# Softmax normalisation of the latent-attention heads: from the score tiles to the gate tile

## The chip, the cores and the metric

The kernel runs on one core of one Trainium2 chip. A time is the device time of one execution in microseconds (us); the number given for a kernel is the median over its runs. A profile comes from one execution whose instructions the hardware profiler recorded; its span runs from the first instruction to the end of the last, and that execution's own device time stands beside it. The engines are named as in the profile: PE is the matrix engine (PEld its weight loads), DVE the vector engine, ACT the scalar engine, POOL is GpSimd, and SP issues transfers. The letter q behind an engine's name marks its instruction queue.

## The reference, cut to what matters

The model is an encoder of two layers on 512 tokens of width 1024. The first layer is a neighbourhood attention. The second is a latent attention with 16 heads, in which every query attends to all 512 keys, and whose output is multiplied by a gate before the output projection:

```python
def block_attention(q, k, v):                 # q, k: (B, S, H, 96); v: (B, S, H, 64)
    ...
    s = jnp.einsum('bqhd,bkhd->bhqk', qblk, k).astype(jnp.float32) * scale
    pr = jax.nn.softmax(s, axis=-1).astype(v.dtype)
    return jnp.einsum('bhqk,bkhd->bqhd', pr, v)

def mixer_mla(xn, w_in, q_norm, w_qb, kv_norm, w_kvb, w_out):
    c_q, c_kv, k_rope, z = jnp.split(xn @ w_in, ...)
    ...
    o = block_attention(q, k, v)
    return (o.reshape(B, S, H * MLA_V) * jax.nn.silu(z)) @ w_out
```

The softmax divides each row of exponentials by its sum. That sum belongs to one query and one head, so dividing the scores, dividing the head's output, or dividing the gate of that head and query all give the same product.

## The kernel before, in words

Everything is 32-bit. A matrix product is made of three products of rounded operands: each operand is split into a high part (a copy rounded on ACT) and a remainder (a subtraction on DVE or POOL). `mms` (line 123) issues such matmuls, `split` (lines 110 and 112) makes the two parts of a tile that comes out of a matmul or a transpose, and `load_w` (lines 99 to 101) loads a weight tile with a transfer on SP, makes the high part on ACT and the remainder on POOL, or on DVE where the caller asks for it.

The second layer's attention is `mla_heads`. It first makes the eight gate tiles `zs[j]` of 128 x 512 (`z_phase`, silu on ACT at line 190). Tile j has the 128 output columns of the head pair j as partitions and the 512 tokens as columns: partitions 0 to 63 belong to the even head, 64 to 127 to the odd head. Then it walks through 70 steps. Step i below 64 is one score tile: head i // 4, query block i % 4, so that a head pair is eight steps. In a step come, in this order,

- `score(i)`: three matmuls into a PSUM tile (bank "S"), the negated row maximum on DVE (line 1052), the exponential on ACT with the row sums accumulated (line 1054), the reciprocal of the sums on DVE (line 1055) and the product of the 128 x 512 tile `ex` with that reciprocal on POOL (line 1056);
- pieces of preparation for later heads (`queries`, `keys`, `values`, `rope`, weight loads), and in the last pair a second product of the layer (`ple`, whose tiles are stored to DRAM at line 1138);
- `turn(i - 3)`: four transposes of an older `ex` (line 155) and their split into `pt_hi` and `pt_lo`;
- in two of four steps `output(h, s)`: the matmuls of the head's values with the turned scores (line 1071), a whole head being done in step 4h + 9. Then `half_of` (lines 220 and 221) puts the two halves of the PSUM tile together in the tile `u` of the pair, and after the odd head `gated` multiplies `u` by `zs[j]` on POOL (line 225), copies the high part on ACT (line 228) and makes the remainder on POOL (line 229). These are `o1h` and `o1l`.

The output projection (`out_proj`) is the next stage. It runs through the pairs in chunks of two, the last pair in the last chunk, and reads its weights (`mla_o`), the residual rows (line 1251) and the norm's gains (line 148) by transfers on SP.

A score tile `ex` has four buffers, `u` two, the raw weight tiles three, the split weight tiles three. The order of PE's work is written by hand: each piece of a step is issued behind the last matmul of the piece before it (`issue_after`). On the other engines and on SP the order is planned when the program is built, with a timeline that estimates when each operand is there; on the chip each engine's queue then runs strictly in that order.

Of the kernel before, what the change touches and what calls it, by code (L numbers as in the profile page):

```python
# [13 lines left out]
F32 = mybir.dt.float32  # L14
F32R = mybir.dt.float32r
AF = mybir.ActivationFunctionType
ALU = mybir.AluOpType
AX = mybir.AxisListType
PSUM = bass.MemoryType.PSUM
P = 128  # L20
S = 512
# [19 lines left out]
class InOrder:  # L41

    def __init__(self, tc, engine):
        self.tc, self.engine, self.last = tc, engine, None
# [12 lines left out]
class Trunk:  # L57
    def __init__(self, tc, ctx, a, dbg=None):
        self.tc, self.nc, self.a = tc, tc.nc, a
        self.dbg = dbg or {}  # L60
        nc = self.nc
        ec = ctx.enter_context
        self.act, self.dve = nc.scalar, nc.vector
        self.const = ec(tc.tile_pool(name="const", bufs=1))
        self.big = ec(tc.tile_pool(name="big", bufs=8))
        self.zp = ec(tc.tile_pool(name="zp", bufs=8))
        self.wp = ec(tc.tile_pool(name="wp", bufs=4))
        self.ps = ec(tc.tile_pool(name="ps", bufs=2, space=PSUM))
        self.half = self.const.tile([P, 1], F32, name="half")
        self.ident = self.const.tile([P, P], F32, name="ident")  # L70
        nc.vector.memset(self.half, -0.5)
        self.small = ec(tc.tile_pool(name="small", bufs=8))
        self.rows = [[self.const.tile([P, NT], F32, name=f"row{n}{l}") for n in "abcd"] for l in range(2)]
        self.wx, self.wxn = None, 0
        dram = ec(tc.tile_pool(name="dram", bufs=4, space=bass.MemoryType.DRAM))
        self.spill = [dram.tile([P, D], F32, name=f"spill{t}") for t in range(NT)]
        self.pe = [[dram.tile([P, D], F32, name=f"pe{l}{t}") for t in range(NT)] for l in range(2)]
        self.quarter = {}
        self.sums = [{p: dram.tile([2 * P, D], F32, name=f"sum{l}{p}") for p in (4, 5, 6, 7)} for l in range(2)]

    def bigtile(self, name):
# [860 lines left out]
    def mla_heads(self, pool, xT, cT, sets, oT):  # L942


        nc, a = self.nc, self.a
# [90 lines left out]
                self.split(dst[0][r], dst[1][r], psk[r])  # L1036
            A["k", j] = self.last_copy

        EX, ST, PT, U = {}, {}, {}, {}

        def score(i):
            h, qt = i // 4, i % 4
            st = sets[h // 2 % 2]
            q, k, kk = ((st["qe"], st["ke"], 96), (st["qo"], st["ko"], 128))[h % 2]
            if qt == 0:
                ST[h] = [self.small.tile([P, 4], F32, name=n, tag=n) for n in ("mx", "sm", "rc")]
            mx, sm, rc = (t[:, qt:qt + 1] for t in ST[h])
            sp = self.psum("S")
            Q = lambda s: q[s][0:kk, qt * P:(qt + 1) * P]
            K = lambda s: k[s][0:kk, :]  # L1050
            self.mms(sp, [(Q(0), K(0)), (Q(0), K(1)), (Q(1), K(0))])
            nc.vector.reduce_max(mx, sp, axis=AX.X, negate=True)  # L1052
            ex = EX[i] = pool.tile([P, S], F32, name="ex", tag="ex", bufs=4)
            nc.scalar.activation(ex, sp, AF.Exp, bias=mx, accum_out=sm)  # L1054
            nc.vector.reciprocal(rc, sm)  # L1055
            nc.gpsimd.tensor_tensor(out=ex, in0=ex, in1=rc.to_broadcast([P, S]), op=ALU.mult)  # L1056

        def turn(i):
            h, qt = i // 4, i % 4
# [80 lines left out]
        zs = self.z_phase(a["mla_z"], xT, range(NEARLY))  # L1140
# [11 lines left out]
        for i in range(70):  # L1152
            work = []
            if i < 64:
                work.append(lambda: score(i))
                work += pieces(i // 8)[i % 8]
            elif i < 68:
                work.append(ple)
            if 3 <= i < 67:
                work.append(lambda: turn(i - 3))  # L1160
            if i >= 8 and i % 4 < 2:
                work.append(lambda: output(i // 4 - 2, i % 4))
            for f in work:
                with self.tc.issue_after(self.last_mm.ins):
                    f()
            if i == 53:
                last = self.last_mm
# [307 lines left out]
```

## Time and profile before

| | us |
|---|---|
| median of 3 runs | 653.36 |
| lowest and highest run | 652.73, 653.73 |
| the profiled execution's own time | 653.56 |
| its span | 651.5 |

The mean granted clock of PE in the profiled execution was 0.995. The page of the profile gives the busy time of each engine, the span in 40 slices, the transfers, the chain of work that ended last, and the costliest groups of instructions: line, engine, operation, output and inputs, count, then busy time, mean duration of one, and the idle time of the engine just before them with what ended it. Other views answer for a stretch of the span: who waited for whom, an engine's instructions in order of time (start, duration, engine, line), or the busy time of each engine in several stretches.

### The profile page before, as it was taken

Reading aid. Unit: us, or ns where it says so; the run is one execution under the profiler, and the core shown is the slowest. Engines: PE = TensorE matmul, PEld = TensorE weight load, DVE = VectorE, ACT = ScalarE, POOL = GpSimd, SP = SyncE. Lnnn points to the kernel's source line nnn. Section 1 sums busy time; section 2 is a strip of 40 time slices with the busy share of each in tenths; the row PEclk is TensorE's granted clock in tenths of the full one; section 3 lists DMA queues with packets and bytes.
Section 4 is the critical chain, followed back from the end, with each engine's and each line's share of the span. In section 5 each row is a group of like instructions: output and inputs, shape, how many; then the busy total and the mean of one; then the engine's idle time right before and its main releaser. Section 6 shows DMA issues by size and latency. Waiting matters only on the chain.

```text
span 651.5 us, 9980 instructions
## 1 busy us (share of the span) xinstructions
PE 640.2 (98%) x3299; PEld 541.9 (83%) x3299; DVE 427.7 (66%) x886; ACT 453.4 (70%) x903; POOL 408.4 (63%) x371
## 2 busy tenths in 40 slices
PE   9999999999999999999999999999999999999994
PEld 6888878888888888888999887888888888888884
DVE  6197987565665616569715514898988885474665
ACT  7575766887886733788644535897989897547855
POOL 0471006877978853797655516786969887437974
PEclk9999999999999999999999999999999999999997
DMA  9939725778958989446643245120112223683524
GB/s 326 355 124 306 217 66 179 263 205 217 229 209 217 239 178 342 147 154 188 224 140 102 78 109 156 32 75 24 49 50 66 65 84 112 229 292 126 193 65 162
DMA packets 46131, 107.41 MB, mean 165 GB/s; under 512 B 4736, under 2 KB 17792, under 8 KB 46080
## 3 DMA queue, kind: packets, MB, share of 16 engines
q1 hardware_dynamic: 34608, 87.12, 39.3%
q0 software_dynamic: 11040, 18.88, 13.6%
q10 hardware_dynamic: 432, 0.79, 0.3%
q8 instruction: 26, 0.43, 0.3%
q14 instruction: 25, 0.20, 0.1%
HBM read 95.23 MB, written 25.17 MB: 185 GB/s over the span
## 4 chain that ended last, share of the span: by engine, by line
PE 83%; POOL 1%; ACT 1%; DVE 0%; DMA 0%; issue 0%; POOLq 0%
PE ps_mm L123 27%; PE ps_S L123 10%; PE ps_mm L959 7%; PE ps_T L155 6%; PE ps_T L851 5%; PE ps_O L1071 5%; PE ps_mm L851 3%; PE ps_S L851 3%; PE ps_O L608 2%; PE ps_T L123 2%; PE ps_O L123 2%; PE ps_mm L909 2%; PE ps_T L301 2%; PE ps_T L596 2%; PE ps_S L909 1%; PE ps_S L559 1%
## 5 line engine op out<-in xcount | busy, mean ns | idle before, releaser
L101 POOL TENSOR_TENSOR wwlo<-wraw,wwhi 128x1024 fp32r<-128x1024 f32 (+5 forms) x68 | 122.3, 1810 | 93.5 <-ACT wwhi L100 41.9
L796 POOL TENSOR_TENSOR wlo<-wraw,whi 128x512 fp32r<-128x512 f32 x56 | 72.7, 1331 | 22.3 <-ACT whi L794 20.2
L1056 POOL TENSOR_TENSOR ex<-ex,rc 128x512 f32<-128x512 f32 x64 | 66.2, 1043 | 26.6 <-DVE rc L1055 22.5
L100 ACT ACTIVATE wwhi<-wraw 128x1024 fp32r<-128x1024 f32 (+5 forms) x71 | 55.1, 799 | 34.3 <-PE ps_mm L123 18.9
L1054 ACT ACTIVATE ex<-ps_S,mx 128x512 f32<-128x512 f32 x64 | 44.0, 687 | 12.6 <-DVE mx L1052 10.9
L1052 DVE TENSOR_REDUCE mx<-ps_S 128x1 f32<-128x512 f32 x64 | 43.7, 683 | 8.4 <-PE ps_S L123 7.7
L582 POOL TENSOR_TENSOR ex<-ex,rc 128x128 f32<-128x128 f32 (+1 forms) x64 | 37.5, 701 | 17.7 <-DVE rc L578 17.5
L112 DVE TENSOR_TENSOR pt_lo<-ps_T,pt_hi 128x512 fp32r<-128x512 f32 x64 | 43.1, 680 | 7.1 <-ACT pt_hi L110 6.7
L110 ACT ACTIVATE pt_hi<-ps_T 128x512 fp32r<-128x512 f32 x64 | 37.7, 594 | 3.4 <-PE ps_T L155 3.0
L155 PE MATMUL ps_T<-ident,ex 128*128 128x128 f32 x256 | 38.3, 272 | 0.0
L155 PEld LDWEIGHTS ps_T<-ident,ex 128*128 128x128 f32 x256 | 31.5, 140 | 7.5
L123 PE MATMUL ps_mm<-xh,wwhi 128*128 128x512 f32 x120 | 33.7, 404 | 0.0
L221 DVE TENSOR_TENSOR u<-ps_O,u 64x512 f32<-64x512 f32 x32 | 21.9, 685 | 17.7 <-ACT u L220 17.2
L576 ACT ACTIVATE ex<-ex,mx 128x128 f32<-128x128 f32 (+1 forms) x64 | 30.2, 473 | 4.2 <-DVE mx L565 4.1
L123 PE MATMUL ps_mm<-xl,wwhi 128*128 128x512 f32 x120 | 31.9, 395 | 0.0
L794 ACT ACTIVATE whi<-wraw 128x1024 fp32r<-128x1024 f32 x28 | 29.3, 1057 | 3.2 <-DMA wraw<-sum 2.4
L123 PE MATMUL ps_mm<-xh,wwlo 128*128 128x512 f32 x120 | 31.1, 394 | 0.0
L123 PE MATMUL ps_S<-ke,qe 96*128 96x512 f32 x96 | 28.9, 407 | 0.3 <-DMA qe<-rl 0.3
L123 PE MATMUL ps_S<-ko,qo 128*128 128x512 f32 x96 | 28.9, 409 | 0.0
L959 PE MATMUL ps_mm<-cT,wwhi 128*128 128x512 f32 x94 | 27.7, 393 | 0.0
L220 ACT ACTIVATE u<-ps_O 64x512 f32<-64x512 f32 x32 | 18.9, 591 | 12.0 <-PE ps_O L608 8.8
L225 POOL TENSOR_TENSOR u<-u,z 128x512 f32<-128x512 f32 x16 | 22.6, 1412 | 7.5 <-DVE u L221 7.5
(488 smaller groups left out, 1915.1 us busy)
## 6 DMA issues: line engine op xcount, KB each, us to landing
sum<-gate POOLq DMA_DIRECT2D x12, 1024.0 KB, 8.2
wraw<-na_qk SPq DMA_DIRECT2D x16, 512.0 KB, 4.9
wraw<-sum SPq DMA_DIRECT2D x16, 512.0 KB, 3.3
pe<-pe SPq DMA_DIRECT2D x31, 256.0 KB, 5.9
wraw<-gate SPq DMA_DIRECT2D x12, 512.0 KB, 3.3
wraw<-na_v SPq DMA_DIRECT2D x10, 512.0 KB, 3.4
sum<-sum POOLq DMA_DIRECT2D x4, 1024.0 KB, 11.1
wraw<-na_o SPq DMA_DIRECT2D x8, 512.0 KB, 4.8
```

The source lines that it names most:

```text
L100: nc.scalar.activation(hi[:, c], raw[:, c], AF.Copy)
L101: f = lambda e, c=c: e.tensor_tensor(out=lo[:, c], in0=raw[:, c], in1=hi[:, c].bitcast(F32), op=ALU.subtract)
L110: self.last_copy = self.act.activation(hi, src, AF.Copy, scale=scale)
L112: self.dve.tensor_tensor(out=lo, in0=src, in1=hi.bitcast(F32), op=ALU.subtract)
L123: last = self.last_mm = nc.tensor.matmul(out, l, r, start=i == 0, stop=i == n - 1)
L155: self.last_mm = self.nc.tensor.transpose(t[:, i * P:(i + 1) * P], b, self.ident)
L796: nc.gpsimd.tensor_tensor(out=lo[:, o], in0=raw[:, o], in1=hi[:, o].bitcast(F32), op=ALU.subtract)
L851: mm = nc.tensor.matmul(ps, l, r, start=j == 0 and p in banks, stop=j == 11 and p in (2, 3, 4), skip_group_check=True)
L959: self.last_mm = nc.tensor.matmul(PS[key], *terms[i], start=i == 0, stop=i == len(terms) - 1)
L1052: nc.vector.reduce_max(mx, sp, axis=AX.X, negate=True)
L1054: nc.scalar.activation(ex, sp, AF.Exp, bias=mx, accum_out=sm)
L1056: nc.gpsimd.tensor_tensor(out=ex, in0=ex, in1=rc.to_broadcast([P, S]), op=ALU.mult)
```

## The change

In the second layer's heads the score tiles are no longer multiplied. The eight sums of a head pair (two heads, four query blocks) are collected in one tile of 128 x 8. After the last score of the pair, the new function `weigh(j)` takes the reciprocal of that tile in one DVE instruction and stores it with one transfer on SP into a DRAM tensor `inv[j]` of 2 x 512, which means 1024 separate elements of four bytes, because consecutive DRAM elements come from different partitions. Two more transfers on SP read it back into the tile `rows` of 128 x 512: the 512 inverse sums of the even head as the same row in partitions 0 to 63, those of the odd head in partitions 64 to 127. Last, POOL multiplies `zs[j]` by `rows` in place. `turn`, `output` and `gated` are as they were.

```diff
+        self.inv = [dram.tile([2, S], F32, name=f"inv{j}") for j in range(8)]
...
         def score(i):
             h, qt = i // 4, i % 4
...
             if qt == 0:
-                ST[h] = [self.small.tile([P, 4], F32, name=n, tag=n) for n in ("mx", "sm", "rc")]
-            mx, sm, rc = (t[:, qt:qt + 1] for t in ST[h])
+                ST[h] = self.small.tile([P, 4], F32, name="mx", tag="mx")
+            if i % 8 == 0:
+                SM[i // 8] = [self.small.tile([P, 8], F32, name=n, tag=n) for n in ("sums", "inv")]
+            mx, sm = ST[h][:, qt:qt + 1], SM[i // 8][0][:, i % 8:i % 8 + 1]
...
             nc.scalar.activation(ex, sp, AF.Exp, bias=mx, accum_out=sm)
-            nc.vector.reciprocal(rc, sm)
-            nc.gpsimd.tensor_tensor(out=ex, in0=ex, in1=rc.to_broadcast([P, S]), op=ALU.mult)
+            if i % 8 == 7:
+                weigh(i // 8)
+
+        def weigh(j):
+            sm, inv = SM.pop(j)
+            nc.vector.reciprocal(inv, sm)
+            d = self.inv[j]
+            at = lambda off, ap: bass.AP(tensor=d.tensor, offset=d.offset + off, ap=ap)
+            nc.sync.dma_start(at(0, [[1, P], [P, 8]]), inv)
+            rows = pool.tile([P, S], F32, name="rows", tag="rows", bufs=2)
+            for e in range(2):
+                nc.sync.dma_start(rows[64 * e:64 * e + 64], at(e * S, [[0, 64], [1, S]]))
+            nc.gpsimd.tensor_tensor(out=zs[j], in0=zs[j], in1=rows, op=ALU.mult)
```

More of the change, by code (lines that the diff above doesn't have):

```diff
@@ L1037, in keys @@
             A["k", j] = self.last_copy
-        EX, ST, PT, U = {}, {}, {}, {}
+        EX, ST, PT, U, SM = {}, {}, {}, {}, {}
         def score(i):
```

## The prediction

> **What bounds the kernel now.** I read the page first, then the busy times by stretch, then what PE itself waited for, then the chain of waits inside the heads.
>
> ```profile
> span 651.5 us, 9980 instructions
> PE 640.2 (98%) x3299; PEld 541.9 (83%) x3299; DVE 427.7 (66%) x886; ACT 453.4 (70%) x903; POOL 408.4 (63%) x371
> ...
> core 0: us, PE busy (x) PEld busy (x) DVE busy (x) ACT busy (x) POOL busy (x), PEclk, DMA share, GB/s
> 381.00:403.00 22.00, 21.70 (x96) 17.66 (x95) 6.14 (x10) 10.10 (x17) 9.36 (x8) 1.00 0.48 133
> 403.00:561.00 158.00, 158.00 (x866) 133.07 (x865) 127.11 (x253) 132.51 (x290) 121.28 (x111) 1.00 0.22 68
> 561.00:582.00 21.00, 21.00 (x101) 17.51 (x100) 13.21 (x12) 7.34 (x9) 8.63 (x5) 1.00 0.91 337
> 642.00:651.50 9.50, 0.79 (x7) 0.59 (x5) 4.52 (x12) 3.86 (x9) 1.67 (x3) 0.65 0.55 204
> ```
>
> The heads run from 403 to 561. In these 158.00 us PE is busy 158.00 us at a granted clock of 1.00; POOL, which the change relieves, is busy 121.28 us. PE's idle time of the whole span is 651.5 - 640.2 = 11.3 us, and 8.71 of it is the tail behind the last matmuls, which the change does not touch. What PE waited for around the heads (395 to 570):
>
> ```profile
> PE ps_S L123 <- DMA qe<-rl: 0.3, 1, 0.3
> ...
> PEld ps_S L123 <- DMA qe<-rl: 0.7, 1, 0.7
> ```
>
> One wait, of 0.3 us in the matmuls and 0.7 us in the weight loads, for a transfer that feeds the first head. No matmul or weight load waited for `ex`.
>
> But a busy PE in this profile can hide short stalls, because a matmul's recorded end is modelled and the records overlap. So I compare the pace with a stretch in which no score tile is consumed:
>
> ```profile
> 431.08 0.94 PE ps_O L1071 x4
> ...
> 562.86 5.89 PE ps_mm L123 x26
> ...
> L155 PEld LDWEIGHTS ps_T<-ident,ex 128*128 128x128 f32 x256 | 31.5, 140 | 7.5
> ```
>
> In the chain of waits, four matmuls of a head take 0.94 us, 235 ns each; 26 of the output projection take 5.89 us, 227 ns each. The 256 transposes of `ex`, which are the instructions that would wait for POOL's product, have 7.5 us of weight-load idle time between them, 29 ns each, and no releaser is named. That is the pipeline's own spacing. PE therefore sets the time in the heads, and its own work stays the same.
>
> [...]
>
> **The change, part by part.**
>
> ```profile
> L1056 POOL TENSOR_TENSOR ex<-ex,rc 128x512 f32<-128x512 f32 x64 | 66.2, 1043 | 26.6 <-DVE rc L1055 22.5 <-PE ps_S L123 2.4 <-PE ps_O L1071 1.6
> L1055 DVE RECIPROCAL rc<-sm 128x1 f32<-128x1 f32 x64 | 10.1, 158 | 11.4 <-ACT ex L1054 10.7
> L225 POOL TENSOR_TENSOR u<-u,z 128x512 f32<-128x512 f32 x7 | 9.1, 1293 | 1.4 <-DVE u L221 1.4
> L101 POOL TENSOR_TENSOR wwlo<-wraw,wwhi 128x512 fp32r<-128x512 f32 (+3 forms) x24 | 28.4, 1202 | 9.1 <-ACT wwhi L100 9.0
> ```
>
> Removed on POOL: 64 products, 66.2 us. Added: 8 products of two full 128 x 512 inputs, for which the `u` by `z` product is the row: 8 x 1.293 = 10.3 us. POOL falls from 121.3 to about 65 us in the heads. On DVE 64 reciprocals (10.1 us) become 8; a 128 x 8 one I cost like the 128 x 1 one, 0.16 us, so 8.8 us fall away. The waits in those rows (22.5 us of POOL for the reciprocal, 10.7 of DVE for the exponential) go too. What is late next on the way score, exponential, turn is PE itself. All of this lies beside PE: worth 0 us, bounds 0 and a gain of 0.3, the one wait of PE in this stretch, although that one lies ahead of the first pair's sums. The transposes now wait for ACT instead of POOL; in the trace they found `ex` ready even one engine later.
>
> Added on SP: 8 stores and 16 loads.
>
> ```profile
> q1 hardware_dynamic: 34608, 87.12, 39.3%
> ...
> qe<-rh SPq DMA_DIRECT2D x8, 64.0 KB, 1.9
> ...
> ko<-slab_h SPq DMA_DIRECT2D x2, 128.0 KB, 2.3
> ko<-slab_l SPq DMA_DIRECT2D x2, 128.0 KB, 3.2
> ...
> 506.49 0.51 SPq L117 DMA_DIRECT2D qe<-rh  x1
> ```
>
> An issue costs SP about 0.51 us (the row of `qe`), so 24 cost 12 us in 158, off PE's path. The load of one half of `rows` writes 128 KB, as `ko<-slab` does: 2.3 to 3.2 us to landing. The trace shows no store of 4-byte elements. Its lower bound is the quickest small transfer, 1.9 us. For the upper bound let each of the 1024 elements cost as much as the mean packet of q1: 39.3% of 16 engines' 651.5 us over 34608 packets is 118 ns, 64 packets per engine make 7.6 us, and 1.9 + 7.6 = 9.5 us. I take 4 us, nearer to the small transfers, since q1's mean packet carries 2.5 KB. The Trainium skill, "DMA: Bandwidth & Descriptors", section "Rules for kernel authors", says that a strided last dimension is cut into one descriptor per element, which is where a count of 1024 would come from; no run so far shows it.
>
> From the pair's last sums to the weighted gate tile: reciprocal 0.16, issue 0.51 and store 4 (1.9 to 9.5), two issues 1.02 and the second load 2.8 (2.3 to 3.2), one POOL instruction in front at most 2.40 (the 128 x 1024 remainder below), product 1.29. Without that instruction the lower end is 0.16 + 0.51 + 1.9 + 1.02 + 2.3 + 1.29 = 7.2, with it the upper end is 18.1, and the value I take is 9.8 us. The last pair has least time:
>
> ```profile
> 549.21 0.16 DVE L1055 RECIPROCAL rc<-sm 128x1 f32<-128x1 f32 x1
> ...
> 550.78 1.29 POOL L229 TENSOR_TENSOR o1l<-u,o1h 128x512 fp32r<-128x512 f32 x1
> 559.33 2.40 POOL L101 TENSOR_TENSOR wwlo<-wraw,wwhi 128x1024 fp32r<-128x1024 f32 x1 [7.26 <-ACT wwhi L100]
> 562.70 1.29 POOL L225 TENSOR_TENSOR u<-u,z 128x512 f32<-128x512 f32 x1 [0.97 <-DVE u L221]
> 564.73 1.29 POOL L229 TENSOR_TENSOR o1l<-u,o1h 128x512 fp32r<-128x512 f32 x1 [0.74 <-ACT o1h L228]
> 566.63 2.73 POOL L101 TENSOR_TENSOR ww<-wraw,ww 128x1024 fp32r<-128x1024 f32 x1 [0.61 <-ACT ww L100]
> 575.47 2.59 POOL L101 TENSOR_TENSOR ww<-wraw,ww 128x1024 fp32r<-128x1024 f32 x1 [6.10 <-ACT ww L100]
> ...
> 571.76 0.41 PEld L123 LDWEIGHTS ps_mm<-ww,o1l 128*128 128x128 f32 x2
> ...
> 579.47 0.41 PEld L123 LDWEIGHTS ps_O<-ww,o1h 128*128 128x128 f32 x2
> ```
>
> The last reciprocal starts at 549.21 and the gate product at 562.70: 13.5 us, against 9.8. POOL stands idle for 7.26 us of them, which is where the new product fits. Even if it came late, the remainder `o1l` ends at 564.73 + 1.29 = 566.02 and PE first loads this chunk's `o1l` from 571.76: another 5.7 us. So the last pair affords 19.2 us, more than the upper end of 18.1. Step 8j + 7 holds a pair's last score and step 8j + 13 its last output in every pair, and the earlier pairs' results are read later still by the output projection. Cost: 0.
>
> The new waits and what stands behind them: SP waits for the reciprocal, then for the store's landing before it issues the two loads. Behind it in SP's order stand weight loads and the moves of the next pair's rope rows. A hold of 0.5 to 1 us more than the store's 1.9 to 9.5 us comes eight times. In the heads this falls on weights that reach PE through POOL's 24 remainders (28.4 us), which no longer queue behind 64 products: an instruction at POOL waits for fewer others by 56 us in all, against eight holds of about 4 us. I cost it 0, with 0 to 2 us as bounds. POOL waits for `rows` in its order; behind it stand remainders, rope products and the gate.
>
> The sum: 653.56 (the profiled execution) - 0 + 0 = 653.56. That is 0.2 above the median of 653.36, so against the median I say 653.4.
>
> **The rivals.** *Slower: the last pair's rows come late.* SP's order is planned, not found on the chip, and a store planned too far back stands behind loads that wait for buffers.
>
> ```profile
> 547.15 11.49 SPq L1138 DMA_DIRECT2D pe<-pe  x4
> 559.11 2.98 SPq L99 DMA_DIRECT2D wraw<-mla_o  x2
> 562.18 1.82 SPq L1251 DMA_DIRECT2D r<-spill  x4
> 564.04 0.47 SPq L148 DMA_DIRECT2D gp<-ple_norm  x1
> ```
>
> If the last store goes out behind the two `mla_o` loads, at 562.1, and lands after 1.9 to 9.5, the loads follow after 1.02 and land 2.3 to 3.2 later: 567.3 to 575.8. Product, gate, high part and remainder (1.29 + 1.29 + 0.74 of idle + 1.29, the high part lying in that idle) end at 571.9 to 580.4, against 571.76: 0.1 to 8.6 us late. It decides once `rows` lands after 571.76 - 4.61 = 567.15. The middle, 4 us, gives 657.4. A smaller form: the store held late delays the next `mla_o` transfer; its remainder ends on POOL at 578.06 and PE loads that chunk from 579.47, so 1.4 us are hidden and the rest is paid. For it: the transfers are busy 0.91 of 561 to 582. Against: the sums are ready 12 us before the stretch fills, and two buffers of `rows` let SP run on. Chance 0.18.
>
> *Faster: the weight-load headroom is real.* If the 24.9 us that PEld lies idle in the heads were stalls on late score tiles, the removed products would return them: 653.4 - 24.9 = 628.5. Against it stand the equal pace and the one named wait. Chance 0.02. A gain by a luckier order of PE's neighbours, up to the 11.3 - 8.7 = 2.6 us of idle time outside the tail, gives 650.8; nearly all of it lies ahead of the heads, where nothing is changed: 0.05.
>
> *The change does not do what it says:* the products go, but POOL, in order, stands still for the rows instead. That costs POOL time, not PE's, and gives 653.4 too; it is inside the forecast.
>
> **How the numbers follow.** About 0.2%, 1.3 us, is what a measurement of this kernel can tell from no change. No change 0.75, slower 0.18 (0.1 to 8.6 us; about 657.4), faster 0.07. The forecast's own range is 652.1 to 654.7. That holds 0.75 alone; up to 657.0 it takes in almost half of the slower cases, and 651.9 is where the faster ones begin. So 651.9 to 657.0 holds about 0.83.
>
> **What would show it.** Right: POOL near 65 us busy from 403 to 561 and PE still at 158.0 of 158 with no releaser at the transposes of `ex`; the heads end at the same 561; the last store is issued within 2 us of the last reciprocal and `rows` lands before 562; `o1l` of the last pair ends before PE reads it. Wrong: idle time of PE at the output projection with the last pair's `o1h`, `o1l` or a `ww` as releaser; a store landing later than 9.5 us; or a shorter stretch of the heads at the same count of matmuls, which would mean that the busy PE had been waiting.

## The result, and the profile after

The changed kernel is slower. Its median is 688.62 us (687.81 to 689.23, 4 runs) against 653.31 us (652.73 to 653.73, 4 runs) before: 35.3 us more, a ratio of 1.054 (1.0522 to 1.0559). The profiled execution took 689.08 us, its span is 687.3 us. Line numbers of the changed kernel are one higher than before up to the heads, and 14 higher behind the new function: `ps_S` at L124 was L123, the outputs `ps_O` at L1085 were L1071.

First the page, its first lines and its packet count.

```profile
span 687.3 us, 9835 instructions
PE 647.4 (94%) x3299; PEld 546.4 (79%) x3299; DVE 422.1 (61%) x830; ACT 453.6 (66%) x903; POOL 353.8 (51%) x315
...
DMA packets 55731, 109.54 MB, mean 159 GB/s; under 512 B 13312, under 2 KB 26368, under 8 KB 55680
```

PE runs the same 3299 matmuls, but it was idle for 687.3 - 647.4 = 39.9 us where it had been idle for 11.3, and its busy time grew by 7.2 us. These are 28.6 + 7.2 = 35.8 us, the whole difference of the two spans (687.3 - 651.5). Next the busy times by stretch; the columns are those of the prediction's stretches (engine busy us and count, then granted clock, DMA share, GB/s).

```profile
403.00:430.00 27.00, 26.50 (x148) 22.20 (x146) 18.88 (x31) 19.19 (x44) 5.79 (x5) 1.00 0.19 52
430.00:460.00 30.00, 22.62 (x122) 19.36 (x123) 19.81 (x32) 21.15 (x47) 7.43 (x7) 0.89 0.23 58
460.00:490.00 30.00, 23.41 (x121) 19.42 (x121) 18.76 (x31) 19.55 (x44) 15.26 (x14) 0.89 0.26 71
490.00:520.00 30.00, 30.00 (x165) 25.11 (x164) 24.24 (x41) 24.82 (x57) 11.32 (x10) 1.00 0.14 32
520.00:550.00 30.00, 21.56 (x116) 18.17 (x115) 16.87 (x28) 17.74 (x38) 8.82 (x7) 0.89 0.25 62
...
403.00:598.00 195.00, 167.90 (x885) 139.96 (x883) 122.89 (x197) 132.90 (x291) 65.71 (x55) 0.95 0.27 67
```

The lost time does not lie evenly. 490 to 520 is as full as before, while each 30 us stretch shown with a granted clock of 0.89 lacks 43 to 49 of its 165 matmuls. Who waited for whom (engine, tile and line, releaser; us in total, times, longest):

```profile
POOL z L1070 <- DMA rows<-inv: 79.2, 7, 14.0
...
ACT rh L998 <- POOL rl L997: 25.0, 4, 9.0
...
PE ps_S L124 <- ACT ex L1057: 15.0, 2, 8.4
...
POOL z L1070 <- PE ps_S L124: 10.4, 1, 10.4
...
PE ps_S L124 <- DVE mx L1055: 7.9, 1, 7.9
...
PE ps_mm L124 <- POOL wwlo L102: 4.4, 1, 4.4
```

Read from the top, this is already the chain: POOL stands 79.2 us for `rows`; ACT stands 25.0 us for the rope tile `rl` of POOL; PE stands for `ex` of ACT. Two names mislead. The 10.4 us that POOL spends at the seventh product, put down to PE, are a wait for `rows` too: the second of its loads lands at 574.75 and the product starts at 574.82. The page gives 89.5 us of idle time ahead of the eight products in all. And the 7.9 us of PE named after `mx` are a wait for `ex`: the maximum of the score tile that PE overwrites there was taken at 425.81, its exponential ran at 436.55, and the weight load of that matmul names `ex` of ACT. The timeline around the first pair shows each link: start, duration, engine, line, operation, and in brackets the engine's idle time and what ended it.

```profile
418.06 0.38 SPq L1066 DMA_DIRECT2D inv<-inv  x1
...
421.38 1.30 POOL L996 TENSOR_TENSOR rl<-rl,rope_s 128x512 f32<-128x512 f32 x1
...
426.83 1.12 SPq L1069 DMA_DIRECT2D rows<-inv  x2
...
428.33 1.17 PE L1085 MATMUL ps_O<-pt_hi,vt 128*128 128x512 f32 x4
432.12 1.26 POOL L1070 TENSOR_TENSOR z<-z,rows 128x512 f32<-128x512 f32 x1 [9.44 <-DMA rows<-inv]
433.34 1.26 POOL L997 TENSOR_TENSOR rl<-rh,rl 128x512 f32<-128x512 f32 x1
434.64 0.63 ACT L998 ACTIVATE rh<-rl 128x512 fp32r<-128x512 f32 x1 [8.99 <-POOL rl L997]
...
436.55 0.69 ACT L1057 ACTIVATE ex<-ps_S,mx 128x512 f32<-128x512 f32 x1
...
437.38 1.65 PE L124 MATMUL ps_S<-ko,qo 128*128 128x512 f32 x3 [7.88 <-DVE mx L1055]
```

The store goes out at 418.06, the loads at 426.83, and the product on `z` starts at 432.12. It stands in POOL's order between the two halves of a rope (L996 and L997) that multiply and add the next heads' queries. ACT's copy `rh` needs the second half, and behind that copy in ACT's order stands the exponential that would release the score tile. PE's four matmuls from 428.33 on are its last until 437.38. Nobody needed `z` by then: the gate product of this pair (L226) starts at 443.32.

This happens at pairs 0, 2 and 4, where a rope comes next; the distance between PE's neighbouring starts gives stalls of 8.0, 6.8 and 8.6 us there, and one of 1.4 us behind pair 5. The last pair has the fifth, of 4.6 us, behind a weight remainder:

```profile
595.87 1.26 POOL L1070 TENSOR_TENSOR z<-z,rows 128x512 f32<-128x512 f32 x1 [14.04 <-DMA rows<-inv]
597.09 2.34 POOL L102 TENSOR_TENSOR wwlo<-wraw,wwhi 128x1024 fp32r<-128x1024 f32 x1
...
599.48 1.22 PE L124 MATMUL ps_mm<-wwlo,o1h 128*128 128x512 f32 x2 [4.43 <-POOL wwlo L102]
...
601.78 1.05 PE L124 MATMUL ps_mm<-wwhi,o1h 128*128 128x512 f32 x2
602.64 1.05 PE L124 MATMUL ps_mm<-wwhi,o1l 128*128 128x512 f32 x2
...
605.25 0.62 PE L124 MATMUL ps_S<-wwhi,o1h 128*128 128x512 f32 x2
605.70 0.62 PE L124 MATMUL ps_S<-wwhi,o1l 128*128 128x512 f32 x2
```

The same lines show the second loss. At 601.78 two matmuls take 0.86 us from start to start, 430 ns each; at 605.25 they take 0.45 us, 225 ns each. After each of the four long stalls the records hold a half granted clock for 6.8 us (from 433.6, 481.4, 529.2 and 597.4), partly while PE stands and partly while it works. In these four stretches PE is busy for 14.1 us; at the full clock the same work would take half of that, an estimate of 7.1 us lost, which is nearly all of the 7.2 us of added busy time. The Trainium skill, "TensorE: Matmul & The Clock Gate", section "Part 1: The HAM clock gate (the "warmup" mystery)", says that an idle array falls to half rate and returns to the full one after about 3.4 us of sustained work. The trace agrees in kind: here the full pace was back some 4.8 us after the end of the stall at 599.48.

And the reason for the long wait, the landing times of the eight stores (L1066) and, in the second view, of the sixteen loads (L1069):

```profile
DMA to landing us min/median/max: 8.4/8.9/11.9
```

```profile
DMA to landing us min/median/max: 2.7/4.4/5.4
```

It is not the packets themselves that take so long. The transfers from 418 to 428, in 40 slices of 0.25 us (the busy share of the 16 DMA engines, in tenths), around the store that goes out at 418.06:

```profile
DMA  0000773000000000000000000000000000000000
...
DMA packets 1040, 0.00 MB, mean 0 GB/s; under 512 B 1040, under 2 KB 1040, under 8 KB 1040
...
inv<-inv SPq DMA_DIRECT2D x1, 4.0 KB, 8.7
```

All packets of this store are recorded between 419.0 and 419.75, and then no DMA engine has a packet for the 7 us until it lands. What passes in these 7 us the records do not show.

### The profile page after: what moved, and what is told of

Read it like the earlier page. It is cut to its first block, busy times and chain, and to the rows that moved or that the text cites. A ratio compares the mean times of both kernels' runs of the same rounds, so it can differ in the third digit from the quotient of the medians.

```text
span 687.3 us, 9835 instructions
## 1 busy us (share of the span) xinstructions
PE 647.4 (94%) x3299; PEld 546.4 (79%) x3299; DVE 422.1 (61%) x830; ACT 453.6 (66%) x903; POOL 353.8 (51%) x315
## 2 busy tenths in 40 slices
DMA packets 55731, 109.54 MB, mean 159 GB/s; under 512 B 13312, under 2 KB 26368, under 8 KB 55680
## 4 chain that ended last, share of the span: by engine, by line
PE 67%; DMA 9%; POOL 4%; ACT 2%; issue 2%; DVE 1%; SPq 0%; POOLq 0%; ACTq 0%; DVEq 0%
PE ps_mm L124 25%; PE ps_S L124 8%; DMA inv<-inv 6%; PE ps_T L156 4%; PE ps_mm L960 4%; PE ps_mm L852 3%; PE ps_T L852 3%; DMA rows<-inv 3%; PE ps_S L852 2%; PE ps_O L1085 2%; PE ps_O L609 2%; PE ps_T L124 2%; PE ps_O L124 2%; PE ps_mm L910 2%; PE ps_T L597 1%
## 5 line engine op out<-in xcount | busy, mean ns | idle before, releaser
L101 ACT ACTIVATE wwhi<-wraw 128x1024 fp32r<-128x1024 f32 (+5 forms) x71 | 55.1, 799 | 33.9 <-PE ps_mm L124 18.9
L1070 POOL TENSOR_TENSOR z<-z,rows 128x512 f32<-128x512 f32 x8 | 10.2, 1277 | 89.5 <-DMA rows<-inv 79.2
L124 PE MATMUL ps_S<-ko,qo 128*128 128x512 f32 x96 | 31.2, 436 | 22.9 <-ACT ex L1057 15.0
L124 PEld LDWEIGHTS ps_S<-ko,qo 128*128 128x128 f32 x96 | 17.5, 201 | 26.7 <-ACT ex L1057 24.2
L124 PE MATMUL ps_mm<-xh,wwhi 128*128 128x512 f32 x120 | 33.7, 404 | 0.0
L124 PE MATMUL ps_mm<-xl,wwhi 128*128 128x512 f32 x120 | 31.9, 395 | 0.0
L226 POOL TENSOR_TENSOR u<-u,z 128x512 f32<-128x512 f32 x16 | 22.6, 1413 | 17.6 <-DVE u L222 17.5
L795 ACT ACTIVATE whi<-wraw 128x1024 fp32r<-128x1024 f32 x28 | 29.3, 1057 | 2.9 <-DMA wraw<-sum 2.0
L124 PE MATMUL ps_mm<-xh,wwlo 128*128 128x512 f32 x120 | 31.1, 394 | 0.0
L124 PE MATMUL ps_S<-ke,qe 96*128 96x512 f32 x96 | 28.9, 408 | 0.0
```

The lines of the kernel that those rows point to most:

```text
L101: nc.scalar.activation(hi[:, c], raw[:, c], AF.Copy)
L124: last = self.last_mm = nc.tensor.matmul(out, l, r, start=i == 0, stop=i == n - 1)
```

## The experiments

Theory A: the store of 1024 four-byte pieces lands late, POOL stands in order in front of rope and remainders, and PE starves through ACT. Rivals: SP's hold delays weights and rope rows (B); the undivided scores or the newly planned order cost by themselves (C); the last pair's rows alone are late (D, the prediction's slower rival; the trace above already has four of the five stalls ahead of the last pair's); the small packets disturb other transfers (E). All ratios are to the kernel before, on the same chip as the experiment.

**The removal alone.**

```diff
-            if i % 8 == 7:
-                weigh(i // 8)
```

> Leaves out the division altogether: no reciprocal, no store, no loads, no product with the gate tile; only the removal of the 64 products and 64 reciprocals is left of the change. Theory A (the store of 4-byte elements lands late and POOL, in order, stands still at the gate tile's product with rope additions and weight remainders behind it): 653 +- 1.5, PE's stalls of 5 to 9 us gone. Theory B (SP's queue, held 8 to 12 us for each store, makes moves and weights late): the same, 653. Theory C (undivided scores or the newly planned order cost by themselves): 680 to 690.

Measured 653.04 us, ratio 0.9999 (0.9989 to 1.0008). The heads of this kernel in the stretch of the prediction:

```profile
403.00:561.00 158.00, 157.91 (x864) 132.69 (x863) 120.65 (x188) 131.88 (x289) 57.50 (x47) 1.00 0.22 69
```

POOL's 121.28 us became 57.50 and PE did 864 matmuls instead of 866. Taking away 64 products and 64 reciprocals is worth nothing, so all of the 35.3 us belong to what was added, and undivided scores cost nothing by themselves.

**The transfers alone**, with the score tiles divided as before and nothing that reads `rows`.

```diff
+            inv = SM[i // 8][1][:, i % 8:i % 8 + 1]
+            nc.vector.reciprocal(inv, sm)
+            nc.gpsimd.tensor_tensor(out=ex, in0=ex, in1=inv.to_broadcast([P, S]), op=ALU.mult)
...
-            nc.vector.reciprocal(inv, sm)
...
-            nc.gpsimd.tensor_tensor(out=zs[j], in0=zs[j], in1=rows, op=ALU.mult)
```

> The products on the score tiles are back; the store and the two loads of each pair stay, but nothing reads the loaded rows, so no engine but SP waits for them. Theory A: 653 to 657, although the stores still land after 8 to 12 us. Theory B: 675 to 690, with PE waiting for moved rope rows or weights that stand behind the store in SP's queue. Theory C: 653.

Measured 652.57 us, ratio 0.9996 (0.9984 to 1.0008). SP's wait in this kernel:

```profile
SPq L1071 <- DMA inv<-inv: 71.8, 8, 10.3
```

SP was held as long as in the change (70.2 us there), the packets were all there (55731), and it cost nothing. That ends B and E.

**The same mathematics, with the rows multiplied onto the output.** `rows` is kept, and `output` multiplies `U[j]` by it just ahead of the gate.

```diff
-            nc.gpsimd.tensor_tensor(out=zs[j], in0=zs[j], in1=rows, op=ALU.mult)
+            RW[j] = rows
...
+                nc.gpsimd.tensor_tensor(out=U[j], in0=U[j], in1=RW.pop(j), op=ALU.mult)
```

> All of the change, but POOL multiplies the rows into u, just ahead of the gate product, instead of into the gate tile: POOL reaches that instruction some 14 us later, since it needs u. Theory A: 653 to 662; POOL waits little for the rows, the stalls at the scores of the pairs 1, 3 and 5 (8.0, 6.8, 8.6 us) are gone, the last pair may still stall. Theory B: 680 to 690, as SP is held as long as in the change. Theory C: 680 to 690.

Measured 652.89 us, ratio 0.9996 (0.9987 to 1.0006). The waits of this kernel:

```profile
POOL u L1094 <- DMA rows<-inv: 5.1, 1, 5.1
...
SPq L1069 <- DMA inv<-inv: 72.1, 8, 10.3
```

The store is as slow as before (8.7 to 11.7 us to landing), but the product also depends on `u`, which is finished six steps later. It stands at another place in POOL's order, and POOL waits 5.1 us for `rows` instead of 89.5. The whole change, with the product at the other factor of the gate, costs nothing. This speaks for A alone: neither the transfers nor the late rows cost, but the place of the instruction that waits for them.

**The size of the pieces.** Three stores of the same 4 KB in longer pieces. The store line in pieces of 32, 16 and 8 bytes:

```diff
-            nc.sync.dma_start(at(0, [[1, P], [P, 8]]), inv)
+            nc.sync.dma_start(at(0, [[8, P], [1, 8]]), inv)
...
+            nc.sync.dma_start(at(0, [[4, P], [4 * P, 2], [1, 4]]), inv.rearrange("p (a b) -> p a b", b=4))
...
+            nc.sync.dma_start(at(0, [[2, P], [2 * P, 4], [1, 2]]), inv.rearrange("p (a b) -> p a b", b=2))
```

> The store writes 128 pieces of 32 bytes instead of 1024 of 4 bytes, in another order of the inverse sums, so that the rows hold the right numbers in the wrong places; all else, and the order on PE, DVE, ACT and POOL, as in the change. Theory A: the store lands after 2 to 3 us instead of 8.4 to 11.9, POOL's waits fall from 7 to 14 us to 2 to 6 us each, 655 to 665. Theory B: also 655 to 665, because SP's hold shrinks alike. Theory C: 685 to 690. If the number of pieces does not set the store's time: 688.

> As the 8-byte store, with 256 pieces of 16 bytes (rows again in the wrong order). Theory A: landing after 2.4 us, stalls 6.3 us shorter than in the change, 1.7, 0.5 and 2.3 us left: 653 to 659. Theory A': 685 to 690.

> The store writes 512 pieces of 8 bytes (the inverse sums of two query blocks side by side, so the rows are in the wrong order); the order on PE, DVE, ACT and POOL is that of the change. Theory A with a time per piece: 1024 pieces landed after 8.7 us and 128 after 1.4, 8.1 ns a piece, so 512 land after 4.5 us; the rows come 4.2 us sooner than in the change and each of its stalls of 8.0, 6.8, 8.6, 1.4 and 4.6 us is 4.2 us shorter (11.1 left), plus some time at the half clock: 662 to 669. Theory A' (a threshold: below some size a piece costs as much as a 4-byte one, whatever the count): 685 to 690.

Measured: 32 bytes 653.13 us, 1.0001 (0.9992 to 1.0011); 16 bytes 653.34 us, 1.0004 (0.9995 to 1.0013); 8 bytes 657.2 us, 1.0076 (1.0059 to 1.0094). Landing times of the store with pieces of 32 bytes, then 16, then 8:

```profile
DMA to landing us min/median/max: 1.4/1.4/1.4
```

```profile
DMA to landing us min/median/max: 1.6/2.2/3.3
```

```profile
DMA to landing us min/median/max: 3.0/3.7/4.6
```

In all four kernels PE, DVE, ACT and POOL have the same instructions in the same order, so only the landing time differs. At 32 bytes the change's own planned order costs nothing, which ends what was left of C; the time is even below the 655 to 665 us expected, because POOL's waits of 18.9 us for `rows` hold up none of PE's matmuls. The landing time is hidden at 1.4 and at 2.2 us, shows at 3.7 and is ruinous at 8.9. The 8-byte kernel's waits and heads:

```profile
POOL z L1070 <- DMA rows<-inv: 29.3, 7, 6.9
...
PE ps_S L124 <- ACT ex L1057: 3.0, 3, 1.4
```

```profile
403.00:561.00 158.00, 154.69 (x846) 129.18 (x845) 120.29 (x195) 130.31 (x288) 64.21 (x53) 1.00 0.27 77
```

The same three places stall, for 0.8, 1.1 and 1.6 us by the distance of PE's starts, 3.5 us together. The 662 to 669 us expected of it were too many: stalls this short did not halve the clock (1.00 in the heads), and most of POOL's 29.3 us of waiting is hidden.

**The same product on DVE.**

```diff
-            nc.gpsimd.tensor_tensor(out=zs[j], in0=zs[j], in1=rows, op=ALU.mult)
+            nc.vector.tensor_tensor(out=zs[j], in0=zs[j], in1=rows, op=ALU.mult)
```

> All of the change, the 4-byte store too, but the gate tile is multiplied by the rows on DVE instead of POOL. Theory A (the price is what stands behind the instruction that waits): DVE is now held, with the row maxima and the remainders of the turned scores behind it, which every score and every transpose needs, so all eight pairs stall PE, not five: 700 to 770. If POOL itself, its rope additions or its memory accesses were the cause: 653 to 665.

Measured 730.08 us, ratio 1.1181 (1.1164 to 1.1198). Its waits:

```profile
DVE z L1070 <- DMA rows<-inv: 79.7, 8, 11.4
PE ps_S L124 <- ACT ex L1057: 52.5, 8, 8.4
```

The wait is no longer than POOL's 89.5 us, but on DVE the maxima and remainders of every pair's scores stand behind it: eight stalls instead of five, and 77 us instead of 35.

**The store turned on PE first**, so that it has 8 pieces of 512 bytes. PE turns `inv`, DVE copies it, and the call stands at the second step of the next pair.

```diff
+            t = self.psum("T")
+            self.last_mm = nc.tensor.transpose(t[0:8, 0:P], inv, self.ident)
+            turned = pool.tile([P, P], F32, name="turned", tag="turned", bufs=1)
+            nc.vector.tensor_copy(turned[0:8], t[0:8, 0:P])
+            nc.sync.dma_start(at(0, [[P, 8], [1, P]]), turned[0:8])
```

> The change with the eight columns of inverse sums turned on PE into eight rows (one more transpose and one copy on DVE per pair, two steps later), so that the store writes 8 pieces of 512 bytes. Theory A: the store lands after about 2 us and nothing waits: 652.5 to 655, that is, the time of before, since PE's work is 0.9 us longer and the removed POOL work lies beside it. If the idea itself costs time: 660 or more.

Measured 654.99 us, ratio 1.0033 (1.0021 to 1.0045). Its waits:

```profile
POOL z L1072 <- DMA rows<-inv: 46.3, 8, 9.5
...
PE ps_T L1065 <- DVE pt_lo L113: 1.1, 2, 0.6
```

Most of the loss is gone. What is left, 2.0 us, has 1.1 us of named waits at two of the eight added turns on PE, which is the engine without slack. POOL still stands 46.3 us, and in the heads no wait of PE has POOL as its releaser. The loads go out 1.2 to 3.4 us behind the store. But the later call also puts the rope's addition ahead of the product in POOL's order (422.96 and 428.63 at the first pair), so this run does not separate the quick landing from the better place.

**Rope ahead of the product.** The product's statement goes to `output` as in the third experiment, still on `z`, and for pairs 0, 2 and 4 it is ordered behind the rope's last instruction.

```diff
+                with self.tc.issue_after(A["rl", j // 2 + 1].ins) if j in (0, 2, 4) else nullcontext():
+                    nc.gpsimd.tensor_tensor(out=zs[j], in0=zs[j], in1=RW.pop(j), op=ALU.mult)
```

> The change, with one thing moved: in the pairs 0, 2 and 4 POOL's product of the gate tile stands behind the two rope instructions of the next group (lines 997 and 999) instead of ahead of them; store, loads and all other places in POOL's queue as in the change. Theory A: the three stalls of 8.0, 6.8 and 8.6 us and most of their time at the half clock (about 2 us each) go; what stays is 1.4 us at pair 5's weights and 4.6 us at the last pair's, with some time at the half clock: 658 to 664. If the 192-column remainders, which still stand behind the product, matter as well: 664 to 675.

Measured 666.3 us, ratio 1.0198 (1.0181 to 1.0215). POOL around the first pair:

```profile
425.98 1.30 POOL L999 TENSOR_TENSOR rl<-rl,rh 128x512 fp32r<-128x512 f32 x1 [1.23 <-ACT rh L998]
433.10 1.30 POOL L1095 TENSOR_TENSOR z<-z,rows 128x512 f32<-128x512 f32 x1 [5.83 <-DMA rows<-inv]
434.36 1.16 POOL L102 TENSOR_TENSOR wwlo<-wraw,wwhi 128x192 fp32r<-128x192 f32 x2
```

The rope now ends before the wait, and 22 of the 35.3 us are back although POOL still waits 67.9 us for `rows` by name. Its waits of PE:

```profile
PE ps_mm L124 <- POOL wwlo L102: 4.6, 1, 4.6
...
PE ps_mm L960 <- POOL wwlo L102: 3.5, 1, 3.5
```

For the other 13 us the profiled execution, the slowest of the four at 668.37 us, has three stalls by the distance of PE's starts: 1.6 us at pair 4, where ACT waits for the gate product that stands behind the wait, and 3.7 and 4.8 us for weight remainders of 512 and 1024 columns that stand behind it, followed by 3.4 and 6.8 us of half clock. The time lies above the 658 to 664 us expected. It falls within the 664 to 675 us given for the case that the 192-column remainders matter, but none of the three stalls is at one of these.

**Rope on DVE.** POOL's three rope instructions move, the product stays.

```diff
-            (nc.gpsimd if g else nc.vector).tensor_tensor(out=sw, in0=sw, in1=rs_t, op=ALU.mult)
-            nc.gpsimd.tensor_tensor(out=sw, in0=xr, in1=sw, op=ALU.add)
+            nc.vector.tensor_tensor(out=sw, in0=sw, in1=rs_t, op=ALU.mult)
+            nc.vector.tensor_tensor(out=sw, in0=xr, in1=sw, op=ALU.add)
...
-            A["rl", g] = nc.gpsimd.tensor_tensor(out=rl, in0=sw, in1=rh.bitcast(F32), op=ALU.subtract)
+            A["rl", g] = nc.vector.tensor_tensor(out=rl, in0=sw, in1=rh.bitcast(F32), op=ALU.subtract)
```

> The change, with the rope instructions of all groups (lines 996, 997, 999) on DVE instead of POOL: the product of the gate tile waits on POOL as long as before, but no rope instruction stands behind it. Theory A: as with the product moved behind them, 658 to 664, with POOL's waits for the rows unchanged at about 80 us in sum. If POOL's waiting costs through anything else, or DVE becomes too full: 670 to 690.

Measured 663.01 us, ratio 1.0158 (1.0143 to 1.0173). Its waits:

```profile
POOL z L1070 <- DMA rows<-inv: 90.6, 8, 13.7
...
PE ps_mm L124 <- POOL wwlo L102: 4.0, 1, 4.0
PE ps_mm L960 <- POOL wwlo L102: 1.7, 1, 1.7
```

POOL stands as long as in the change, 90.6 us against 89.5, and yet 25 of the 35.3 us are back, since the rope no longer stands behind it. The length of the wait does not tell its price.

**The statement later, without an order.** The product on `z` is written ahead of the gate, as in the third experiment, and nothing else is asked.

```diff
-            nc.gpsimd.tensor_tensor(out=zs[j], in0=zs[j], in1=rows, op=ALU.mult)
+            RW[j] = rows
...
+                nc.gpsimd.tensor_tensor(out=zs[j], in0=zs[j], in1=RW.pop(j), op=ALU.mult)
```

> The change, with the statement of the gate tile's product moved in the program from the end of the pair's scores to just ahead of the gate product, six steps later, and no order asked for. The planned order on POOL comes out as in the change (product ahead of the rope instructions), because the plan takes the rows to be there early. Theory A: 684 to 690, nothing gained. If the place of the statement decides: 653 to 662.

Measured 691.21 us, ratio 1.0588 (1.0566 to 1.061), a little above what was expected. Its waits:

```profile
PE ps_S L124 <- ACT ex L1057: 23.4, 3, 8.1
```

The planner puts the product at the same early place in POOL's order. The third experiment was cured by its dependence on `u`, not by the line on which it is written.

## Why the prediction was wrong, point by point

*PE bounds the heads and the removed work is worth 0:* right. The removal alone gave a ratio of 0.9999, and POOL's busy time in the heads was foretold at about 65 us and measured at 65.71 (403 to 598). The rival by the weight loads' busy share (24.9 us of headroom) is refuted by the same run. The Trainium skill, "Perfetto Trace Analysis", section "Identifying the Most-Contended Engine", asks for the matmul work done as a share of the peak rate and for the weight loads' busy share as the measures of PE's headroom. The weight loads' share alone would have misled here: they are busy 132.69 of 158 us without the 64 products, and nothing came back of the 25 us that look free.

*The store: bounds 1.9 to 9.5 us, 4 taken:* mis-sized. The median was 8.9 us, and the longest, 11.9, lies above the bound. The row that came nearest is the one that I set aside, 118 ns for each of 64 pieces per engine, but it came near by luck: the packets of the first store are all recorded within 0.75 us, and the time passes between the last of them and the landing. The count of 1024 is shown by the packets: per pair 1072 more packets under 512 B than before with 4-byte pieces ((13312 - 4736) / 8), and 176 with 32-byte pieces ((6144 - 4736) / 8). The difference, 896, is 1024 - 128 pieces. This agrees with the Trainium skill, "DMA: Bandwidth & Descriptors", section "Rules for kernel authors", which gives one descriptor per element for such a last dimension. The loads took 4.4 us instead of 2.8 in the median.

*SP's hold at 0:* right; held 71.8 us in the second experiment, at no cost.

*"That costs POOL time, not PE's":* this is the step that failed. The prediction listed what stands behind POOL's wait, "remainders, rope products and the gate", and then priced the wait by POOL's slack. It did not follow each of these to its reader. The rope feeds ACT, in whose order the exponentials follow, and PE cannot write the next scores until an exponential has released a score tile. The rows of four kernels show that the length of a wait is no measure:

| kernel | who stood | for the transfer, us | longer than before, us |
|---|---|---|---|
| transfers alone | SP | 71.8 | -0.5 |
| the change | POOL | 89.5 | 35.3 |
| rope on DVE | POOL | 90.6 | 10.0 |
| product on DVE | DVE | 79.7 | 77.1 |

Mis-sizing alone would have been harmless: with the same landing times the product on `u` costs nothing. With a store of 1.4 or 2.2 us the same order costs nothing either. It took both errors, and with the 4 us that I took the time would have been nearly right (a landing after 3.7 us gave 657.2 us, just above the range's 657.0), with the step on POOL's wait as wrong as now.

*The slower rival, the last pair's rows late behind other loads of SP:* the sign was right and the place was wrong. The last store went out 0.2 us after its reciprocal, as foretold, so SP's order was not to blame. From that store at 580.21 to the end of the product at 597.13 are 16.9 us, within the 19.2 that I had granted. The stall came through `wwlo`: the prediction counted this remainder of 1024 columns as the instruction in front of the product, and in the run it stood behind it (597.09). It is 4.4 us of PE's waits; the rope's three places gave 15.0 + 7.9 us.

*What would make it wrong:* a landing beyond 9.5 us was named and came. Idle time of PE at the output projection was named with `o1h`, `o1l` or `ww` as releaser, and came with `wwlo`. The larger stalls, inside the heads, were in no sign of being wrong; they broke the sign of being right, a PE that stays busy for 158.0 of 158 us. PE's half clock after a stall was not in the sum: 7.2 of 35.8 us.

What stays open: that the planner takes these transfers for short is argued only. Shown is that its order on the four compute engines did not change between pieces of 4 and 32 bytes. Why a store of short pieces lands so long after its last packet stays open too.

## What to carry to other kernels

When a change adds a wait for a transfer to an in-order engine, list every instruction behind the waiting one until the transfer lands, and follow each to its reader: the engine's own idle time does not price the wait. Attach a late factor to an operand that is itself late (here `u` and not `z`), so that dependence keeps the waiter back, or order it so by hand; writing the statement later did not move it. Store in long pieces where the order of a layout leaves a choice, and take the upper bound of a store whose piece count is known and whose piece length no row has; here the longest landing, 11.9 us, passed even that bound of 9.5 us.

## What the runs showed of the hardware

- A 4 KB store from 128 partitions landed after 1.4 us in 128 pieces, 2.2 in 256, 3.7 in 512 and 8.9 in 1024 (medians). If the pieces spread evenly over 16 engines, a further piece per engine delays the landing by an estimated (3.7 - 1.4) / 24 = 96 ns at 8 bytes and (8.9 - 1.4) / 56 = 134 ns at 4 bytes. This time lies behind the packets: those of the first 4-byte store are recorded within 0.75 us. Why the shortest delay it more each, no run tells.
- The loss of clock has a threshold between the stalls seen: in the 8-byte kernel those of 0.8 to 1.6 us left the granted clock at 1.00, and in the change those of 4.6 to 8.6 us halved it for 6.8 us each. In between, with the rope ahead of the product and with the rope on DVE, stalls of 3.7 and 4.1 us halved it for 3.4 us each.
- The transfers themselves, 9600 packets more in the span, slowed nothing that could be measured (0.9996).
